# Compressing the prompt's blocks together with the last cached chunk, and re-measured durations in the build-time planner

## The chip, the cores and the metric

One core of a Trainium2 chip runs the whole program. The metric is the device time of one execution in microseconds (us). The engines are TensorE (PE, with its weight loads listed apart as PEld), VectorE (DVE), ScalarE (ACT), GpSimd (POOL) and SyncE (SP), which issues all DMA transfers here.

## The reference, cut to what matters

The reference runs two layers of a hybrid decoder on a prompt (512 tokens) and on eight samples of four tokens, with shared weights. Per layer:

```python
h = rmsnorm(x, norm_g) * (1 + scale) + shift
u, z_s5, q, kvx, gate_logits, z_nsa, merge_logits = split(h @ w_in)
y5 = s5_scan(u, ...); y5 = gelu(y5); y5 = y5 * sigmoid(y5 @ glu_w + glu_b) * silu(z_s5)
kc = rope(silu((kv_all[0] blocks of 64 + pe) @ cmp_w1[0]) @ cmp_w2[0])   # compressed keys
vc =      silu((kv_all[1] blocks of 64 + pe) @ cmp_w1[1]) @ cmp_w2[1]    # compressed values
o  = gated sum of attention over compressed, selected and window keys
out = (m_s5 * (y5 @ w_s5_out) + m_nsa * ((o * silu(z_nsa)) @ w_nsa_out)) @ w_o
x = x + gate * out
```

For the samples, `kv_all` is 2048 cached rows, read through a page table (16 pages for each of 8 samples and layer), and the new rows. For the prompt it is the prompt's own 512 rows, 8 blocks. One `rmsnorm(x, final_g)` ends the program.

## The kernel before, in words

Activations lie transposed (features on partitions, 512 + 32 tokens along the free axis), cut at token 256 into two halves h = 0 and 1. The wide matrices are split into a high and a low part, and each product is three matmuls. Weight blocks of 128 x 1024 are streamed by DMA (`w_dma`), their high part is cast on ACT (`w_hi`) and the low part subtracted on DVE (`w_lo`), a block ahead of use.

The order of instructions on every engine is fixed at build time. Each piece of work (dense projections, S5 set-up and tiles, compression, attention of the prompt, of the samples, modulation, stores) is a Python generator, a thread with a priority (a lower number goes first; the dense thread has 50, the last). `_Sched.run` resumes the best thread that is ready; what it emits goes to the end of its engine's queue. A thread waits by `yield ev(...)` (something has been emitted), `yield w_` (all that it last emitted is done by the model), or for memory, which `alloc` takes from one arena in SBUF. When things are done is told by a model, `_Clock.note`, which gives each instruction a duration; nothing of these waits exists on the chip, where semaphores alone hold an engine back.

Compression (`compress(l)`): a thread of its own loads the cached pages in eight chunks of 16 pages. For each chunk `products` runs 64 matmuls (32 steps x keys and values) against the resident first weights `cw1`, with 64 columns (4 for each page), 68 in the first chunk, where the encoding `pe` is a 17th page that gives the bias. Then come a bias addition on DVE, a tanh on ACT and `hidden` on DVE. After all chunks `keys` and a value matmul make `kcT` and `vc`. In layer 1 it starts when layer 0's attention is done, and chunk 5 and later ones wait for the end of layer 0.

The prompt's own blocks went separately: dense blocks 14 and 15 (`job_kv`, `post_c`) write the prompt's raw keys and values into four pages `cpage`, and after all projections, in layer 1 also after `compress(1)`, `compress_new(l)` loads `cw1` (2 x 1 MB) and `pe` again, runs the same 64 products with 20 columns, and makes `kcbd` and `vcbd`. The prompt's attention (`prompt`) waits for both, for the projections and for `cmp`.

`s5_wa`, four times a layer, makes its matrices with six DVE operations of 512 columns (a strided operand among them) and then transposes them on PE.

The end: `wo` has eight output blocks; in the last layer `final(h)` multiplies by `final_g` and the reciprocal norm, six blocks on DVE with one scalar_tensor_tensor each, two on POOL after a scaling on DVE, and stores them in pairs.

Of the kernel before, what the change touches and what calls it, by code (L numbers as in the profile page):

```python
# [21 lines left out]
P = 128  # L22
# [81 lines left out]
class _Clock:  # L104
# [41 lines left out]
    def note(self, e, op, args, kw):  # L146
# [44 lines left out]
        elif op == "dma_start":  # L191
            h = self.free[e] = t0 + 0.45
            d = max(self.free.get("dma", 0.0), h + 0.65)
            n = max(x.free_size() * x.ap[0][1] for x in views[:2]) / P if out.space != DRAM else out.free_size() * out.ap[0][1] / P
            end = self.free["dma"] = d + n * 1.42e-3 + 0.01
            vis = end + 0.78
        else:
            extra = 0.061 * sum(1 for x in ins[1:] if x.free_size() == 1) if e == "dve" else 0.0
            if e == "dve":
                c = 0.068 + n * (0.0063 if op == "reciprocal" else 0.00052 if op in ("tensor_scalar", "tensor_copy", "memset") and out.space != PSUM and all(x.space != PSUM for x in ins)  # L200
                                 else 0.00104) + extra
            elif e == "act":
# [88 lines left out]
def body(ctx: ExitStack, tc: tile.TileContext, A, O):  # L291
# [84 lines left out]
    class Ring:  # L376
# [371 lines left out]
    def dense(l):  # L748
# [95 lines left out]
        cpb = q["cpb"] = yield from alloc(5 * 256)  # L844
        cpage = q["cpage"] = cpb.v(5, 2, 32, 4)
# [32 lines left out]
        def job_kv(i):  # L878
            fmb = misc.next()
# [23 lines left out]
            def post_c(h):  # L903
                if h == 0:
                    return
                ty = i - 14
                store(O["kv"][l, ty], fm, fmb)
                for q2 in range(2):
                    ps = psq()
                    for qq in range(2):  # L910
                        qs = slice((2 * q2 + qq) * P, (2 * q2 + qq + 1) * P)
                        tr(ps[:, qq * 256:qq * 256 + P], fm[:, qs])
                        tr(ps[:, qq * 256 + P:qq * 256 + 256], fxs[0][:, qs])

                    pv = ps.rearrange("p (q s g d e) -> p q s g d e", q=2, s=2, g=2, e=2)
                    for d2 in range(2):
                        pr = slice(d2 * 64, d2 * 64 + 64)
                        for half in range(2):
# [205 lines left out]
        def final(h):  # L1124
            a, b = HALVES[h]
            yield ev("rstd", l, h)
            for k in range(8):
# [6 lines left out]
                if k % 2:  # L1134
                    sp.dma_start(O["y"][:, k - 1:k + 1, a:b], yb.v(8, N)[:, k - 1:k + 1, a:b])
        early = (0, 1)
        w = {}
        for m, h in [(m, h) for m in range(6) for h in range(2)] + [(6, 0), (7, 0), (6, 1), (7, 1)]:
# [21 lines left out]
            elif h == 1:  # L1160
                square_acc(acc, xn(m), m)
            if m == 7:
# [5 lines left out]
                else:  # L1168
                    if h == 0:
                        yb = yield from alloc(8 * N)  # L1170
                        for k in early:
                            dve.tensor_scalar(yb.v(8, N)[:, k], xn(k), C["final_g"][:, k:k + 1], None, op0=ALU.mult)
                    S.spawn(final(h), 4, "y")
            yield t()
# [422 lines left out]
    def compress(l):  # L1597
# [3 lines left out]
        kcT, vc, cw2, pbias = q["kcT"], q["vc"], q["cw2"], q["kcb"].v(1, at=1040)  # L1601
        cwb = []
        for _ in range(2):
            cwb.append((yield from alloc(2048, True, keep)))
        cw1 = [b.v(32, 64) for b in cwb]
        ckb = []
        for _ in range(CKB[l]):
            ckb.append((yield from alloc((NPG + 1) * 256, True, keep)))
        hb = yield from alloc(512 + 64 * 2 + 256, True, keep)
        hid = hb.v(8, 2, 32)  # L1610
        xb, th, kt1 = hb.v(64, at=512), hb.v(64, at=576), hb.v(8, 32, at=640)
        for ty in range(2):
            sp.dma_start(cw1[ty], A["cw1"][l, :, ty])

        def loads():
            for c in range(NB):
                if c >= CKB[l]:
                    yield ev("ck", l, c - CKB[l])
                ck = ckb[c % CKB[l]].v(NPG + 1, 2, 32, 4)
                if c == 0:  # L1620
                    sp.dma_start(ck[:, NPG].rearrange("p t d c -> p (t d c)"), A["pe4"][l])
# [5 lines left out]
                yield "for", [], [ck]  # L1627
# [5 lines left out]
        for c in range(NB):  # L1633
            if l > 0 and c == CMP_LATE:
                yield ev("x", l - 1)
            yield ev("ckl", l, c)
            ck = ckb[c % CKB[l]].v(NPG + 1, 2, 32, 4)
            npx = NPG + (c == 0)
            yield from products(ck, cw1, npx, B[7])
            done("ck", l, c)  # L1640
            if c == 0:
                dve.tensor_copy(pbias, B[7][:, 64:65])
            dve.tensor_scalar(xb, B[7][:, 0:64], pbias, None, op0=ALU.add)
            act.activation(th, xb, AF.Tanh, scale=0.5)
            hidden(hid, c, 32, th, xb)
        yield w_
        yield from keys(kcT, kt1, cw2, hid, 0, 8, 32, B[7])
# [7 lines left out]
        for b in ckb + cwb + [hb]:  # L1655
            b.free()
        done("cmp", l)

    def compress_new(l):

        q = L[l]
        yield from compressed_of(l)
        cw2 = q["cw2"]
        kcbd = q["kcbd"] = q["kcb"].v(2, 8, at=512)
        vcbd = q["vcbd"] = q["kcb"].v(8, 64, p=64, at=528)
        if l == 0:
            yield ev("s5m", l)
        cwb = []
        for _ in range(2):
            cwb.append((yield from alloc(2048, True)))  # L1670
        cw1 = [b.v(32, 64) for b in cwb]
        hb = yield from alloc(64 + 32 * 2 + 16 + 64 + 64 + 1, True)
        pbias = hb.v(1, at=272)
        hid, xb, th = hb.v(1, 2, 32), hb.v(32, at=64), hb.v(32, at=96)
        kc, kt1, hrep, vcr = hb.v(1, 8, at=128), hb.v(1, 8, at=136), hb.v(4, 2, 8, at=144), hb.v(64, p=64, at=208)
        for ty in range(2):
            sp.dma_start(cw1[ty], A["cw1"][l, :, ty])
        yield w_
        sp.dma_start(q["cpage"][:, 4].rearrange("p t d c -> p (t d c)"), A["pe4"][l])
        yield w_  # L1680
        yield from products(q["cpage"], cw1, 5, B[4])
        dve.tensor_copy(pbias, B[4][:, 16:17])
        dve.tensor_scalar(xb[:, 0:16], B[4][:, 0:16], pbias, None, op0=ALU.add)
        act.activation(th[:, 0:16], xb[:, 0:16], AF.Tanh, scale=0.5)
        hidden(hid, 0, 8, th, xb)
        yield w_
        yield from keys(kc, kt1, cw2, hid, 0, 1, 8, B[4])
        pool.memset(kcbd, 0.0)
        for g in range(2):
            dve.tensor_copy(kcbd[g * 64:g * 64 + 64, g, :], kc[g * 64:g * 64 + 64, 0, :])  # L1690
        dve.tensor_copy(hrep, hid[:, 0:1, :, 0:8].to_broadcast([P, 4, 2, 8]))
        yield w_
        pe.matmul(B[4][0:64, 0:64], hrep[64:128].rearrange("p r g n -> p (r g n)"), cw2[64:128, 0, :],
                  start=True, stop=True)
        act.activation(vcr, B[4][0:64, 0:64], AF.Copy, scale=0.5)
        dve.tensor_tensor(vcbd, vcr[:, None, :].to_broadcast([64, 8, 64]),
                          C["bd8"][0:64, :, None].to_broadcast([64, 8, 64]), op=ALU.mult)
        for b in cwb + [hb, q["cpb"]]:
            b.free()
        done("kcbd", l)  # L1700
# [385 lines left out]
    def main():  # L2086
# [268 lines left out]
```

## Time and profile before

| what | us |
|---|---|
| median of 3 runs | 1265.72 (1264.18 to 1266.66) |
| profiled execution, its own time | 1271.5 |
| its span | 1269.6 |
| PE busy | 1167.3 |
| DVE busy | 780.0 |
| ACT busy | 473.2 |
| POOL busy | 159.6 |

The mean granted clock of PE is 0.956 of 2.4 GHz. A busy PE is not PE at its peak: at half the clock the same matmuls are busy for twice as long.

### The profile page before, as it was taken

To read this page: it belongs to the slowest core of one execution; us is meant where nothing else is said; L and a number is where in the kernel's file an instruction comes from. 1 tells how busy PE (TensorE), PEld (TensorE's weight loads), DVE (VectorE), ACT (ScalarE), POOL (GpSimd) and SP (SyncE) were. 2 spreads that over 40 slices of the span, in tenths; PEclk is the share of its full clock that TensorE was granted. 3 is DMA by queue.
4 is the path that set the end of the run, shared out by engine and by line. 5 is a ranking of instruction groups with operands and counts; after the bars stand their busy time and mean duration, and the time that the engine had idled before them with its cause. 6 is when DMAs were issued, how large, how long until landed. Compare 5 with 4: busy or idle time off the path is not lost.

```text
span 1269.6 us, 30887 instructions
## 1 busy us (share of the span) xinstructions
PE 1167.3 (92%) x11958; PEld 1057.9 (83%) x11958; DVE 780.0 (61%) x1793; ACT 473.2 (37%) x1122; POOL 159.6 (13%) x335
## 2 busy tenths in 40 slices
PE   5999898998999999999898889899999899999995
PEld 3788897987888888888787889888998778889994
DVE  4686765525666666557234588875756576664744
ACT  4434232313444445532123333242445444443321
POOL 0142242100000000000000232251200000000001
PEclk8999888987999999999899999989999999999997
DMA  9665545765556747259888744645577555723742
GB/s 386 236 197 174 160 129 155 221 230 174 201 151 184 231 126 210 85 207 329 293 302 290 250 129 146 179 124 197 189 216 213 162 185 155 216 77 105 248 128 79
DMA packets 175156, 243.54 MB, mean 192 GB/s; under 512 B 33313, under 2 KB 129826, under 8 KB 172706
## 3 DMA queue, kind: packets, MB, share of 16 engines
q1 hardware_dynamic: 175010, 241.58, 59.6%
q8 instruction: 94, 1.54, 0.5%
q14 instruction: 52, 0.43, 0.1%
HBM read 211.86 MB, written 37.98 MB: 197 GB/s over the span
## 4 chain that ended last, share of the span: by engine, by line
PE 57%; DVE 16%; DMA 13%; SPq 5%; ACT 4%; issue 3%; DVEq 0%; ACTq 0%
PE bank L229 57%; DVE m L229 16%; SPq L229 4%; ACT m L229 3%; DMA m<-in_wblk 2%; DMA m<-in_wo 2%; DMA m<-kpd 1%; DMA m<-in_cmp 1%; DMA m<-in_xT 1%; DMA yd<-m 1%; DMA m<-in_cw 1%; DMA kpd<-m 1%; DMA x_mid<-m 1%; DMA m<-mn 0%; DMA ms<-m 0%
## 5 line engine op out<-in xcount | busy, mean ns | idle before, releaser
L229 PE MATMUL bank<-m,m 128*128 128x288 f32 (+11 forms) x10796 | 1069.2, 282 | 48.7 <-DVE m L229 30.0
L229 PEld LDWEIGHTS bank<-m,m 128*128 128x128 f32 (+4 forms) x10796 | 966.8, 169 | 123.9 <-issue 46.0
L229 DVE TENSOR_TENSOR m<-m,m 128x256 f32<-128x256 f32 (+15 forms) x623 | 382.6, 636 | 163.4 <-ACT m L229 139.6
L229 ACT COPY m<-bank 128x128 f32<-128x128 f32 (+7 forms) x258 | 99.8, 399 | 313.3 <-PE bank L229 300.1
L229 ACT CAST m<-m 128x1024 fp32r<-128x1024 f32 (+7 forms) x274 | 174.9, 650 | 97.8 <-DVE m L229 57.0
L229 PE MATMUL bank<-c_k,m 128*128 128x128 f32 (+1 forms) x590 | 92.8, 281 | 21.8 <-DVE m L229 19.9
L229 ACT ACTIVATE m<-m 128x64 f32<-128x64 f32 (+6 forms) x76 | 35.2, 469 | 172.9 <-DVE m L229 164.9
L229 PEld LDWEIGHTS bank<-c_k,m 128*128 128x128 f32 x590 | 67.8, 145 | 34.2 <-DVE m L229 25.3
L229 ACT ACTIVATE m<-bank 128x256 f32<-128x256 f32 (+3 forms) x130 | 49.9, 389 | 88.4 <-PE bank L229 83.7
L229 POOL TENSOR_TENSOR m<-m,m 128x32 f32<-128x32 f32 (+4 forms) x100 | 56.2, 581 | 201.5 <-ACT m L229 175.1
L229 POOL CAST m<-m 64x128 fp32r<-64x128 f32 x64 | 24.1, 377 | 453.2 <-ACT m L229 429.9
L229 ACT ACTIVATE m<-bank,m 128x384 f32<-128x384 f32 (+4 forms) x132 | 67.8, 522 | 13.0 <-DVE m L229 13.0
L229 DVE TENSOR_REDUCE m<-bank 128x1 f32<-128x128 f32 (+4 forms) x132 | 57.2, 473 | 16.6 <-PE bank L229 16.1
L229 DVE COPY m<-bank 128x32 f32<-128x32 f32 (+6 forms) x104 | 39.2, 384 | 40.6 <-PE bank L229 22.9
L229 DVE SCALAR_TENSOR_TENSOR m<-m,bank 128x256 f32<-128x256 f32 x96 | 41.4, 433 | 32.6 <-PE bank L229 13.3
L229 DVE SCALAR_TENSOR_TENSOR m<-m,m 128x256 f32<-128x256 f32 (+5 forms) x64 | 28.3, 466 | 45.1 <-ACT m L229 44.6
L229 DVE TENSOR_SCALAR m<-m,m,m 128x128 f32<-128x128 f32 (+4 forms) x132 | 52.5, 439 | 2.5
L229 POOL TENSOR_TENSOR m<-m,c_k 128x256 f32<-128x256 f32 (+2 forms) x32 | 34.0, 1062 | 150.4 <-PE bank L229 150.2
L229 POOL MEMSET m<- 128x32 f32 (+5 forms) x52 | 8.2, 180 | 266.6 <-PE bank L229 179.2
L229 DVE SCALAR_TENSOR_TENSOR m<-bank,mod,m 128x256 f32<-128x256 f32 x32 | 15.2, 480 | 40.7 <-PE bank L229 28.3
L229 ACT ACTIVATE m<-m,m 128x512 f32<-128x512 f32 (+2 forms) x24 | 15.9, 662 | 58.9 <-DVE m L229 53.8
L229 ACT ACT_TABLE_LOAD x24 | 30.8, 1283 | 16.1 <-DVE m L229 15.0
(60 smaller groups left out, 413.7 us busy)
## 6 DMA issues: line engine op xcount, KB each, us to landing
m<-in_wblk SPq DMA_DIRECT2D x78, 512.0 KB, 4.4
m<-in_cmp SPq DMA_DIRECT2D x256, 128.0 KB, 3.5
m<-in_kvsel SPq DMA_DIRECT2D x256, 128.0 KB, 3.0
m<-in_ada_w SPq DMA_DIRECT2D x32, 512.0 KB, 4.8
m<-in_ada_q SPq DMA_DIRECT2D x8, 1024.0 KB, 14.7
m<-in_cw SPq DMA_DIRECT2D x8, 1024.0 KB, 7.5
m<-in_wo SPq DMA_DIRECT2D x16, 512.0 KB, 5.6
ms<-m SPq DMA_DIRECT2D x16, 272.0 KB, 3.1
```

Of the source, the lines that this page charges most:

```text
L229: return f(*args, **kw)
```

## The change

- In the model, DVE's fixed part becomes 0.155 us instead of 0.068 and a column 0.001 (0.0015 where an operand is strided by 8 or more, 0.0019 in a scan, 0.00055 for simple operations from SBUF to SBUF); POOL's fixed part is 0.27 instead of 0.12 and a column 0.0027 instead of 0.0022.
- `compress_new` is gone. `compress` takes chunk buffers of 21 pages instead of 17; the last four are `cpage`, into which dense blocks 14 and 15 write (block 14 waits until that buffer exists). Each chunk buffer gets `pe` once. The last chunk waits for block 15, has 84 columns, and its upper 20 give the prompt's blocks; from them `kcbd` and `vcbd` are made, ahead of the cached `kcT` and `vc`. The buffers are freed one by one.
- At the end, x times `final_g` is made on ACT as each block comes (`scaled`), `final` is a plain tensor_tensor on DVE or POOL, waits until the last output block has been emitted, and stores in the order 2, 4, 0, 6.
- `job_kv` waits until the next two of three scratch buffers are not held by a store.

```diff
-                c = 0.068 + n * (0.0063 if op == "reciprocal" else 0.00052 if op in ("tensor_scalar", "tensor_copy", "memset") and out.space != PSUM and all(x.space != PSUM for x in ins)
-                                 else 0.00104) + extra
+                far = any(abs(x.ap[-1][0]) >= 8 and x.ap[-1][1] > 1 for x in ins)
+                fast = op in ("tensor_scalar", "tensor_copy", "memset") and all(x.space != PSUM for x in [out] + ins)
+                c = 0.155 + extra + n * (0.0063 if op == "reciprocal" else 0.0019 if op == "tensor_tensor_scan" else
+                                         0.00055 if fast else 0.0015 if far else 0.001)
...
-                c = 0.12 + n * (0.0035 if op == "tensor_copy" else 0.0009 if op == "memset" else 0.0022)
+                c = 0.27 + n * (0.0035 if op == "tensor_copy" else 0.0009 if op == "memset" else 0.0027)
...
+        def wait(self, n):
+            while any(self.b[(self.i + 1 + j) % len(self.b)] in kept for j in range(n)):
+                yield t(0.3)
...
+                if i == 15:
+                    done("cp", l)
+            if i == 14:
+                yield ev("ckb", l)
...
-                if k in early:
-                    pool.tensor_tensor(yk, yk, rr[:, a:b], op=ALU.mult)
-                else:
-                    dve.scalar_tensor_tensor(yk, xn(k)[:, a:b], C["final_g"][:, k:k + 1], rr[:, a:b],
-                                             op0=ALU.mult, op1=ALU.mult)
+            yield ev("last", l)
...
+                (pool if k < 2 else dve).tensor_tensor(yk, yk, rr[:, a:b], op=ALU.mult)
...
+        def scaled(m, a, b):
+            act.activation(yb.v(8, N)[:, m, a:b], xn(m)[:, a:b], AF.Identity, scale=C["final_g"][:, m:m + 1])
...
+            last = c == NB - 1
+            if last:
+                yield ev("cp", l)
             yield ev("ckl", l, c)
-            npx = NPG + (c == 0)
+            npx = NPG + 5 if last else NPG + (c == 0)
...
+            n = 84 if last else 64
...
+            if last:
+                hidden(hnew, 0, 8, th[:, 68:84], xb[:, 68:84])
...
+        yield from keys(kc, kt2, cw2, hnew, 0, 1, 8, B[7])
...
+        done("kcbd", l)
...
         yield from keys(kcT, kt1, cw2, hid, 0, 8, 32, B[7])
...
-    def compress_new(l):
...
-            if l:
-                yield ev("cmp", l)
-            S.spawn(compress_new(l), 8, "cmpnew")
```

## Rows read from the trace of the kernel before

**Rows 1.** The page, engines: busy us (share of the span), instructions.
```profile
PE 1167.3 (92%) x11958; PEld 1057.9 (83%) x11958; DVE 780.0 (61%) x1793; ACT 473.2 (37%) x1122; POOL 159.6 (13%) x335
```

**Rows 2.** Busy times by stretch: length, busy by engine, granted clock, DMA share, GB/s.
```profile
72.00:262.00 190.00, 174.49 (x2051) 166.96 (x2052) 118.15 (x204) 60.47 (x114) 55.49 (x94) 0.94 0.58 172
262.00:312.00 50.00, 43.02 (x492) 39.46 (x491) 21.37 (x64) 12.97 (x31) 5.01 (x17) 0.78 0.58 190
312.00:560.00 248.00, 241.80 (x2376) 210.09 (x2375) 155.41 (x403) 111.84 (x317) 9.80 (x28) 0.99 0.53 167
560.00:690.00 130.00, 117.41 (x1516) 107.81 (x1514) 56.58 (x132) 33.35 (x62) 0.31 (x4) 0.96 0.92 314
690.00:905.00 215.00, 196.28 (x1950) 183.03 (x1950) 162.16 (x326) 78.06 (x161) 63.80 (x124) 0.95 0.56 175
905.00:1240.00 335.00, 327.37 (x3052) 296.86 (x3052) 208.78 (x521) 144.34 (x377) 12.71 (x39) 0.99 0.56 172
```

**Rows 3.** Waits, whole program: who waited for whom, us, times, longest.
```profile
PE bank L229 <- DVE m L229: 69.5, 48, 12.1
```

**Rows 4.** Groups of PE's matmuls by shape: busy us, mean ns, idle before them.
```profile
L229 PE MATMUL bank<-m,m 128*64 128x64 f32 x1792 | 56.9, 226 | 5.2 <-DMA m<-in_cmp 5.2
L229 PE MATMUL bank<-m,m 128*64 128x20 f32 x256 | 10.9, 244 | 0.0
L229 PE MATMUL bank<-m,m 128*64 128x68 f32 x256 | 8.0, 223 | 0.6 <-issue 0.4 <-DMA ud<-m 0.2
```

**Rows 5.** Timeline, layer 0, 262 to 276.5 us: start, us, instruction, idle before it.
```profile
262.69 0.81 SPq L229 DMA_DIRECT2D m<-in_cw  x2
263.60 0.38 SPq L229 DMA_DIRECT2D m<-in_wblk  x1
...
273.55 1.04 ACT L229 CAST m<-m 128x1024 fp32r<-128x1024 f32 x1 [10.44 <-DMA m<-in_wblk]
...
274.78 0.23 DVE L229 SCALAR_TENSOR_TENSOR m<-m,m 128x64 f32<-128x64 f32 x1 [6.48 <-ACT m L229]
...
275.06 1.65 PE L229 MATMUL bank<-m,m 64*64 64x256 f32 x8 [2.30 <-DVE m L229]
```

**Rows 6.** Busy times of one stretch of layer 0.
```profile
275.00:295.00 20.00, 19.89 (x219) 17.40 (x220) 7.91 (x18) 2.96 (x8) 2.40 (x13) 0.57 0.41 136
```

**Rows 7.** Timeline of PE: matmuls with an identity that waited for DVE.
```profile
72.18 0.55 PE L229 MATMUL bank<-c_k,m 128*128 128x128 f32 x3 [2.00 <-DVE m L229]
...
846.88 0.23 PE L229 MATMUL bank<-c_k,m 32*32 32x32 f32 x1 [2.28 <-DVE m L229]
862.99 0.55 PE L229 MATMUL bank<-c_k,m 128*128 128x128 f32 x3 [2.10 <-DVE m L229]
```

**Rows 8.** Groups of DVE's operations by shape.
```profile
L229 DVE TENSOR_TENSOR m<-m,m 128x512 f32<-128x512 f32 x56 | 50.8, 933 | 6.0 <-DMA gd<-m 5.3
...
L229 DVE TENSOR_TENSOR m<-m,m 128x288 f32<-128x288 f32 x14 | 6.4, 458 | 2.5 <-ACT m L229 2.2
```

**Rows 9.** Timeline of the end, and the group of the last multiplies.
```profile
1251.35 2.64 PE L229 MATMUL bank<-m,m 128*128 128x288 f32 x18
...
1252.09 3.42 DVE L229 SCALAR_TENSOR_TENSOR m<-m,c_k,m 128x256 f32<-128x256 f32 x6
...
1255.43 0.47 DVE L229 SCALAR_TENSOR_TENSOR m<-bank,mod,m 128x256 f32<-128x256 f32 x1
...
1258.98 0.18 DVE L229 RECIPROCAL rsc<-rsc 128x3 f32<-128x3 f32 x1 [1.73 <-ACT rsc L229]
...
L229 DVE SCALAR_TENSOR_TENSOR m<-m,c_k,m 128x288 f32<-128x288 f32 x6 | 3.8, 701 | 2.0 <-ACT m L229 2.0
```

**Rows 10.** Timeline, layer 1: store of block 15, and compress_new's bias copy and last multiply.
```profile
779.93 0.53 SPq L229 DMA_DIRECT2D out_kv<-m  x1
...
872.31 0.16 DVE L229 COPY m<-bank 128x1 f32<-128x1 f32 x1 [4.74 <-PE bank L229]
...
892.84 0.68 DVE L229 TENSOR_TENSOR m<-m,c_k 64x512 f32<-64x512 f32 x1
```

More of the change, by code (lines that the diff above doesn't have):

```diff
@@ L843, in dense @@
         gtok = q["gtok"] = vtb.v(5, 32, at=1280)
-        cpb = q["cpb"] = yield from alloc(5 * 256)
-        cpage = q["cpage"] = cpb.v(5, 2, 32, 4)
         ropeC, ropeS, swap = C["ropeC"], C["ropeS"], C["swap"]
@@ L878, in job_kv @@
         def job_kv(i):
+            yield from misc.wait(2)
             fmb = misc.next()
@@ L905, in post_c @@
                     return
-                ty = i - 14
+                ty, cpage = i - 14, q["cpage"]
                 store(O["kv"][l, ty], fm, fmb)
@@ L1126, in final @@
             yield ev("rstd", l, h)
-            for k in range(8):
+            yield ev("last", l)
+            for k in (0, 1, 2, 3, 4, 5, 6, 7):
                 yk = yb.v(8, N)[:, k, a:b]
-                if k in early:
-                    pool.tensor_tensor(yk, yk, rr[:, a:b], op=ALU.mult)
-                else:
-                    dve.scalar_tensor_tensor(yk, xn(k)[:, a:b], C["final_g"][:, k:k + 1], rr[:, a:b],
-                                             op0=ALU.mult, op1=ALU.mult)
-                if k % 2:
-                    sp.dma_start(O["y"][:, k - 1:k + 1, a:b], yb.v(8, N)[:, k - 1:k + 1, a:b])
-        early = (0, 1)
+                (pool if k < 2 else dve).tensor_tensor(yk, yk, rr[:, a:b], op=ALU.mult)
+            for k in (2, 4, 0, 6):
+                sp.dma_start(O["y"][:, k:k + 2, a:b], yb.v(8, N)[:, k:k + 2, a:b])
+        def scaled(m, a, b):
+            act.activation(yb.v(8, N)[:, m, a:b], xn(m)[:, a:b], AF.Identity, scale=C["final_g"][:, m:m + 1])
         w = {}
+        if l + 1 == DEPTH:
+            yb = yield from alloc(8 * N)
         for m, h in [(m, h) for m in range(6) for h in range(2)] + [(6, 0), (7, 0), (6, 1), (7, 1)]:
@@ L1161, in dense @@
                 square_acc(acc, xn(m), m)
+            if (m, h) == (7, 1):
+                done("last", l)
             if m == 7:
@@ L1168, in dense @@
                 else:
[L1169 to L1172, printed above, removed]
                     S.spawn(final(h), 4, "y")
+            if l + 1 == DEPTH:
+                if m >= 6:
+                    scaled(m, a, b)
+                elif h == 1:
+                    scaled(m, 0, N)
             yield t()
@@ L1601, in compress @@
         kcT, vc, cw2, pbias = q["kcT"], q["vc"], q["cw2"], q["kcb"].v(1, at=1040)
+        kcbd, vcbd = q["kcbd"], q["vcbd"] = q["kcb"].v(2, 8, at=512), q["kcb"].v(8, 64, p=64, at=528)
         cwb = []
@@ L1607, in compress @@
         for _ in range(CKB[l]):
[L1608 to L1611, printed above, removed]
+            ckb.append((yield from alloc((NPG + 5) * 256, True, keep)))
+        cks = [b.v(NPG + 5, 2, 32, 4) for b in ckb]
+        hb = yield from alloc(512 + 256 + 84 * 2 + 64 + 8 * 2 + 64 * 2, True, keep)
+        hid, kt1 = hb.v(8, 2, 32), hb.v(8, 32, at=512)
+        xb, th = hb.v(84, at=768), hb.v(84, at=852)
+        hnew, kc, kt2, hrep, vcr = (hb.v(1, 2, 32, at=936), hb.v(1, 8, at=1000), hb.v(1, 8, at=1008),
+                                    hb.v(4, 2, 8, at=1016), hb.v(64, p=64, at=1080))
         for ty in range(2):
             sp.dma_start(cw1[ty], A["cw1"][l, :, ty])
+        for ck in cks:
+            sp.dma_start(ck[:, NPG].rearrange("p t d c -> p (t d c)"), A["pe4"][l])
+        q["cpage"] = cks[(NB - 1) % CKB[l]][:, NPG + 1:NPG + 5]
+        done("ckb", l)
         def loads():
@@ L1618, in loads @@
                     yield ev("ck", l, c - CKB[l])
-                ck = ckb[c % CKB[l]].v(NPG + 1, 2, 32, 4)
-                if c == 0:
-                    sp.dma_start(ck[:, NPG].rearrange("p t d c -> p (t d c)"), A["pe4"][l])
+                ck = cks[c % CKB[l]]
                 for i in range(0, NPG, 4):
@@ L1626, in loads @@
                     yield t(PG_LAT)
-                yield "for", [], [ck]
+                yield "for", [], [ck[:, 0:NPG + 1]]
                 yield t(CK_LATE)
@@ L1635, in compress @@
                 yield ev("x", l - 1)
+            last = c == NB - 1
+            if last:
+                yield ev("cp", l)
             yield ev("ckl", l, c)
-            ck = ckb[c % CKB[l]].v(NPG + 1, 2, 32, 4)
-            npx = NPG + (c == 0)
-            yield from products(ck, cw1, npx, B[7])
+            npx = NPG + 5 if last else NPG + (c == 0)
+            if last:
+                yield "for", [], [cks[c % CKB[l]][:, NPG + 1:]]
+            yield from products(cks[c % CKB[l]], cw1, npx, B[7])
             done("ck", l, c)
+            for b in ([ckb[c % CKB[l]]] if c + CKB[l] >= NB else []) + (cwb if last else []):
+                b.free()
             if c == 0:
                 dve.tensor_copy(pbias, B[7][:, 64:65])
-            dve.tensor_scalar(xb, B[7][:, 0:64], pbias, None, op0=ALU.add)
-            act.activation(th, xb, AF.Tanh, scale=0.5)
-            hidden(hid, c, 32, th, xb)
+            n = 84 if last else 64
+            dve.tensor_scalar(xb[:, 0:n], B[7][:, 0:n], pbias, None, op0=ALU.add)
+            act.activation(th[:, 0:n], xb[:, 0:n], AF.Tanh, scale=0.5)
+            if last:
+                hidden(hnew, 0, 8, th[:, 68:84], xb[:, 68:84])
+            hidden(hid, c, 32, th, xb)
+        yield w_
+        yield from keys(kc, kt2, cw2, hnew, 0, 1, 8, B[7])
+        pool.memset(kcbd, 0.0)
+        for g in range(2):
+            dve.tensor_copy(kcbd[g * 64:g * 64 + 64, g, :], kc[g * 64:g * 64 + 64, 0, :])
+        dve.tensor_copy(hrep, hnew[:, 0:1, :, 0:8].to_broadcast([P, 4, 2, 8]))
+        yield w_
+        pe.matmul(B[7][0:64, 0:64], hrep[64:128].rearrange("p r g n -> p (r g n)"), cw2[64:128, 0, :],
+                  start=True, stop=True)
+        act.activation(vcr, B[7][0:64, 0:64], AF.Copy, scale=0.5)
+        dve.tensor_tensor(vcbd, vcr[:, None, :].to_broadcast([64, 8, 64]),
+                          C["bd8"][0:64, :, None].to_broadcast([64, 8, 64]), op=ALU.mult)
+        done("kcbd", l)
         yield w_
@@ L1654, in compress @@
             yield w_
-        for b in ckb + cwb + [hb]:
-            b.free()
+        hb.free()
         done("cmp", l)
-    def compress_new(l):
[L1661 to L1700, printed above, removed]
     def prompt(l):
```

## The prediction

> **What bounds the kernel now.** I read the page's engine table first, then the busy times by stage, PE's waits, and the timeline where PE stands still. The reader is to see that TensorE (PE) is busy nearly all the time [rows 1], so the span is PE's work, plus the stretches in which PE stands still, plus the stretches in which it runs at the lower of its two clock levels. The stage rows [rows 2] separate these. PE's idle time in the six stages is 15.5, 7.0, 6.2, 12.6, 18.7 and 7.6 us, together 67.6. Span times (1 − granted clock) is 11.4, 11.0, 2.5, 5.2, 10.8 and 3.4 us, together 44.3, which is the full-speed time that the 1.2 GHz level takes away. The two go together: the stages with idle time are those with a low clock. The totals of waits say for whom PE stands still: VectorE (DVE) ends 69.5 us of it [rows 3], 12.1 of them at the program's start.
>
> **Part A, the separate compression goes.** Per layer, compress_new loaded 2 x 1 MB of weights and a 128 KB block again and ran 64 products of 20 columns, two records each. In the trace they are 256 records, 10.9 us [rows 4], all in PE's own order, so all of it counts. In exchange the last cached chunk has 84 columns instead of 64. A chunk of 64 takes 56.9/14 = 4.1 us (1792 records, 128 a chunk). If its time grows with the columns, 20 more cost 4.1 x 20/64 = 1.3 us a layer. The 68-column chunks cost 8.0/2 = 4.0, no more than 64 columns, so the other end is 0. I take the dear end: −10.9 + 2.5 = −8.4 us (bounds −10.9 and −8.4). The small matmuls, the tanh and the copies behind the products remain; only their place changes.
>
> **Part B, the stall in layer 0 that the second weight load makes.** The order in the timeline [rows 5]: SyncE issues the two weight loads at 262.69; a dense weight block issued at 263.60, behind them, makes ScalarE (ACT) wait 10.44 us at 273.55; behind that cast stands the tanh of the last chunk, behind the tanh DVE's multiply at 274.78, and behind this the key matmuls, for which PE idles 2.30 us. From 275 to 295 the clock is then 0.57 [rows 6]: 8.6 us of full-speed time lost. Part A already holds some of it: of the 10.9 us, layer 1 can have taken some 4.1 (a whole chunk), so layer 0 took 6.8, 2.7 of them slowness. Remaining: 2.3 + 8.6 − 2.7 = 8.2 us. The loads go, but the key matmuls still stand behind a tanh in ACT's queue. I take two thirds, −5.5 (bounds 0 and −8.2).
>
> **Part C, waits that a wrong duration made.** The emission decides at build time when PE's next instruction may be put into its queue, which runs in order: if it thinks DVE done too early, dense matmuls stand behind a waiting one. The old model gives a 512-column DVE operation 0.068 + 512 x 0.00104 = 0.600 us; measured is 0.933 [rows 8]; the new one gives 0.155 + 512 x 0.0015 = 0.923 when the operand is strided. s5_wa puts six of these ahead of its transposes: the plan is early by 6 x 0.333 = 2.0 us. That is what the trace shows: the waits before those transposes are 2.00 us at 72.18, 2.10 at 862.99 [rows 7], and 2.28, 2.31, 2.08 and 1.10 at the four between, 11.9 us in six. I expect two thirds to go, since the dense blocks can fill the place: −7.9. Of what else waits for DVE, 69.5 − 12.1 − 11.9 − 2.3 (part B) = 43.2 us, such as the 2.28 at 846.88 [rows 7], some is of this kind and some is real dependence, as at the start of attention or at the layer's seam. I take an eighth, −5.4. Together −13.3 (bounds 0 and −11.9 − 43.2/4 = −22.7).
>
> **Part D, the clock behind them.** Outside part B's stage, 60.6 us of idle time goes with 33.3 us lost to the clock [rows 2]. If 13.3 of the 60.6 go, 22% of 33.3 is −7.3 (bounds 0 and, with 22.7, −12.5).
>
> **Part E, the end.** Now the six h = 0 multiplies hold DVE from 1252.09, so the evacuation of the last matmuls, which end at 1251.35 + 2.64 = 1253.99, starts at 1255.43 [rows 9]: 1.4 us late. The change puts those six behind the evacuation, and so ahead of or beside the second rstd, in which DVE idles only 1.73 us before its reciprocal. If they take 3.42 us as now, they cost 3.4 − 1.7 = 1.7. The net is +0.3. The six 288-column multiplies of the last half are 701 ns each beside POOL's two [rows 9], against 458 for the same size elsewhere [rows 8]; a two-operand tensor_tensor beside the same two POOL multiplies I price like the row beside POOL, no gain. The other end is 458 ns: −6 x 0.243 = −1.5 for the last half, and 0.9 less for the first, so bounds −2.1 and +0.3, and I take +0.3. The scaling that moves to ACT lies under wo, where ACT is busy 144 of 335 us [rows 2]; without that cover it would be ten operations, some 5 us. Stores of y: the same eight on SyncE, four of them later; the last still follows the last multiply.
>
> On this one the Trainium skill ("SBUF — State Buffer", section "SBUF: two separate sides") has a rule that speaks against the change. It says that VectorE and GpSimd share one port pair under an exclusive lock, which a VectorE operation with two SBUF inputs needs too while GpSimd reads SBUF, so that one of them stands still. The 701 against 458 ns agrees in direction. By that rule part E is +0.3, without it −2.1.
>
> **Costed at nothing.** The wait of layer 1's last chunk for block 15 is one of the emission's thread, not of an engine: block 15 is stored at 779.93 [rows 10], and until then the dense thread feeds PE. Without that cover it would cost the chunk, 5 us. PE's queue then has dense matmuls behind the chunk, and what it waits for on the chip is the last copies of ACT and DVE, a wait of the 2 us kind. The buffers held until then (weights, one chunk) compete with the S5 tiles for SBUF; counting the allocations I find room for the first tile. Key and value work of the prompt now stands ahead of "cmp", on which the sample, the attention and the second modulation load depend: one chain later. Dense gate blocks hide it; if they ran out it would cost up to the 20 us that it takes beside dense work in layer 1, from 872.31 to 892.84 [rows 10]. The poll in misc.wait (0.3 us a step) is hidden the same way.
>
> **Sum.** B + C + D = −26.1. A new order also makes waits that are not there now; no row sizes them, so their bounds are 0 and all of 26.1. I give back 40%, +10.4: the idle time that the change doesn't touch (60.6 − 13.3 = 47.3) is over three times what it takes away, and its places are drawn anew. −8.4 − 26.1 + 0.3 + 10.4 = −23.8 us. Against the profiled execution, 1271.5 us (span 1269.6), that is 1247.7; the median of the runs is 1265.72, 0.5% less, and from there 1242.
>
> **The rivals.**
> Rival 1: the durations move the order but not the waits; only A and part of B count. −8.4 − 5.5 + 0.3 = −13.6: 1252. For it: most waits on DVE are dependences. Against it: 2.0 us worked out and 2.00 to 2.31 measured.
> Rival 2: nothing is given back, and the far ends of A and E hold: −10.9 − 26.1 − 2.1 = −39: 1227, or lower where more of C goes. For it: six equal waits with one cause. Against it: every order has to fill the same gaps with the same dense blocks.
> Rival 3, slower: in layer 1 the prompt's attention no longer waits for its compressed values, whose last multiply is at 892.84, but starts with the end of the projections at 846.88 [rows 10, 7]. In that stage DVE is busy 162 of 215 us [rows 2], and S5 tiles are still in it. If six of the 32 attention units come to lie in those 46 us, and each stops PE at its two places (transposes behind normalise, the value matmuls behind the copies) by 2.2 us as s5_wa's transposes do, and the clock takes half as much again, that is 12 x 3.3 = 40 us against the 23.8: +16, so 1282. It decides from 23.8/12 = 2 us a place, clock included. Against it: the plan now prices DVE in full and would hold these units back.
> Rival 4: gains and new waits cancel, 1266.
>
> **Chances.** Forecast (own range 1231 to 1249) 0.47; rival 1 0.22; rival 2 0.10; rival 4 0.07; rival 3 0.14. A measurement of this kernel can tell about 0.2% (2.5 us) from no change. Faster by more than that: 0.47 + 0.22 + 0.10 = 0.79; within: 0.07; slower: 0.14. The range 1222 to 1267 takes in rivals 1, 2 and 4 and leaves out rival 3 and the far end of C and D.
>
> **What would show it.** A: no 20-column records, 256 records of 84 columns with 4.1 to 5.4 us per 128. B: no ACT wait of 10 us near 263 to 274, and no 20 us at half clock after it. C: the waits before the four-transpose groups under 0.5 us, and PE's total for DVE near 55. D: the mean clock at 0.965 or above instead of 0.956. E: the last evacuation straight behind its matmuls, and the second reciprocal late by 1 to 2 us. The prediction is wrong if PE's idle time between 72 and 1240 us does not fall by 5 us or more, or if new waits of 2 us stand between 846 and 905.

## The result, and the profile after

Four runs of each: 1244.55 us (1241.83 to 1249.9) after, 1266.19 (1264.18 to 1269.35) before; ratio 0.9837 [0.9805, 0.9869], 21.6 us faster. The forecast was 1242. The profiled execution took 1244.75 us, its span is 1243.0; the page's engine line:

```profile
PE 1142.0 (92%) x11702; PEld 1037.6 (83%) x11702; DVE 780.4 (63%) x1787; ACT 481.5 (39%) x1130; POOL 154.8 (12%) x335
```

Against [rows 1] the span is 26.6 us shorter, PE's busy time 25.3 shorter, and its idle time nearly unchanged (102.3 before, 101.0 now). The 256 matmuls that went are the 20-column records. Most of the rest is clock: span x (1 − mean granted clock) was 1269.6 x 0.044 = 55.9 us and is 1243.0 x 0.033 = 41.0.

Each trace is one execution, and that of before is one with a low clock: 0.956, where its 66 other runs in the experiments below have 0.964 in the mean (0.954 to 0.972). By those runs before loses 44.9 us to the clock and not 55.9. The changed kernel loses 38.5 us in its four runs and 42.2 in six of `old_tail`, which has its order up to the last blocks. So the clock gave 2 to 6 of the 21.6 us, and not the 14.9 that the two traces show.

The forms, to be held against [rows 4], and the four-transpose groups (the last row here; the first row of the second fence is before's):

```profile
L231 PE MATMUL bank<-m,m 128*64 128x64 f32 x1536 | 51.2, 232 | 12.3 <-DMA m<-in_cmp 5.6 <-DMA m<-in_ada_w 5.3 <-issue 1.4
L231 PE MATMUL bank<-m,m 128*64 128x84 f32 x256 | 9.7, 237 | 0.0
L231 PE MATMUL bank<-m,m 128*64 128x68 f32 x256 | 9.6, 246 | 5.4 <-DMA ud<-m 3.5 <-DMA m<-in_cmp 1.9
L231 PE MATMUL bank<-c_k,m 128*128 128x128 f32 x524 | 77.6, 278 | 4.4 <-DVE m L231 2.8 <-ACT m L231 1.4
```

```profile
L229 PE MATMUL bank<-c_k,m 128*128 128x128 f32 x524 | 80.6, 282 | 17.9 <-DVE m L229 16.8 <-ACT m L229 0.7
```

The products together take 70.5 us instead of 75.8. The wait of 128 x 128 transposes for DVE fell from 16.8 to 2.8 us. PE's waits as a whole (us, times, longest; the first row answers to [rows 3]), after and then those of before that are not in [rows 3]; what no engine or transfer ended (1.4 us after, 2.1 before) and 0.2 us of before for `ud` are left out:

```profile
PE bank L231 <- DVE m L231: 48.8, 28, 12.1
PE bank L231 <- ACT m L231: 14.6, 17, 3.3
PE bank L231 <- DMA m<-in_ada_w: 8.0, 5, 5.3
PE bank L231 <- DMA m<-in_cmp: 7.5, 5, 3.3
PE bank L231 <- DMA m<-ud: 4.3, 3, 1.9
PE bank L231 <- DMA ud<-m: 3.5, 1, 3.5
PE bank L231 <- POOL m L231: 2.3, 1, 2.3
PE bank L231 <- DMA m<-kpd: 1.6, 2, 0.8
```

```profile
PE bank L229 <- ACT m L229: 11.4, 15, 3.3
PE bank L229 <- DMA m<-in_cmp: 5.2, 4, 2.2
PE bank L229 <- DMA m<-kpd: 2.5, 3, 1.7
PE bank L229 <- DMA m<-ud: 2.4, 3, 1.5
```

For DVE PE waits 20.7 us less, for DMA 24.9 instead of 10.3, for ACT 3.2 more and for POOL 2.3: 20.1 together, nearly what DVE gave. That is why the idle time did not move.

**Where the time went.** Stages by the clock on the wall no longer hold the same work, so the borders are now events: the first and the last matmul that adds the causal mask in the prompt's attention (two to a unit, 32 units a layer). In order: 72 us to attention of layer 0, that attention, the seam to attention of layer 1, that attention, the rest. Columns: length, PE busy (instructions), granted clock, DMA share, GB/s. Before, then after:

```profile
72.00:323.35 251.35, 228.87 (x2661) 0.90 0.58 177
323.35:547.90 224.55, 218.35 (x2144) 0.99 0.54 168
547.90:911.98 364.08, 332.77 (x3649) 0.96 0.68 223
911.98:1142.27 230.29, 223.03 (x2192) 0.99 0.58 176
1142.27:1269.60 127.33, 112.70 (x883) 0.93 0.45 140
```

```profile
72.00:286.74 214.74, 204.41 (x2513) 0.99 0.62 187
286.74:524.00 237.26, 231.12 (x2290) 0.99 0.60 184
524.00:840.52 316.52, 277.37 (x3046) 0.93 0.66 215
840.52:1130.68 290.16, 281.41 (x2703) 0.99 0.57 172
1130.68:1243.00 112.32, 97.84 (x769) 0.93 0.45 144
```

The lengths can't be compared alone, since dense work moves between stages; what a stage loses can: its idle time, and its length x (1 − clock). Ahead of layer 0's attention the loss was 22.5 + 25.1 = 47.6 us and is 10.3 + 2.1 = 12.4: 35.2 us gained, two thirds of it clock. In the seam it was 31.3 + 14.6 = 45.9 and is 39.1 + 22.2 = 61.3: 15.4 given back. The other stages move by 1 to 2 us. Idle time and clock loss together fall by some 16 us over the span (1.3 + 14.9); the other 10.4 of the 26.6 us are PE's busy time at full clock, of which the products give some 6 (part A below) and the rest has no place.

How far do such losses go without any change of order? Up to 250 us `before_cwlate` (below) issues the same instructions in the same order as before. From 72 to 250 us, in before and then in `before_cwlate`:

```profile
72.00:250.00 178.00, 162.82 (x1944) 0.93 0.57 170
72.00:250.00 178.00, 161.14 (x1978) 0.97 0.58 175
```

The idle time is 15.2 and 16.9 us, the clock loss 12.5 and 5.3. `old_tail` has the order of the changed kernel up to the last blocks; the same two stages in it:

```profile
72.00:284.92 212.92, 202.60 (x2491) 1.00 0.61 189
...
522.84:834.29 311.45, 276.22 (x3046) 0.94 0.66 219
```

They lose 10.3 and 53.9 us, against 12.4 and 61.3. So a stage can differ by some 7 us between two executions of one order, and some 5 of the 35.2 us ahead of attention are of this kind, 7 of them clock less 2 of idle time. The experiments below are read by these two losses; a difference of less than some 8 us between two traces shows nothing by itself.

### The profile page after: what moved, and what is told of

It reads as the page before. It is cut to its first block, busy times and chain, and to the rows that moved or that the text cites. A ratio compares the mean times of both kernels' runs of the same rounds, so it can differ in the third digit from the quotient of the medians.

```text
span 1243.0 us, 30351 instructions
## 1 busy us (share of the span) xinstructions
PE 1142.0 (92%) x11702; PEld 1037.6 (83%) x11702; DVE 780.4 (63%) x1787; ACT 481.5 (39%) x1130; POOL 154.8 (12%) x335
## 4 chain that ended last, share of the span: by engine, by line
PE 69%; DMA 11%; DVE 7%; ACT 4%; SPq 4%; issue 2%; POOL 0%; DVEq 0%; ACTq 0%; POOLq 0%
PE bank L231 69%; DVE m L231 7%; SPq L231 3%; ACT m L231 3%; DMA m<-in_cmp 2%; DMA m<-in_cw 2%; DMA yd<-m 1%; DMA m<-in_ada_w 1%; DMA m<-kpd 1%; DMA m<-ud 1%; DMA m<-yd 1%; DMA m<-in_s5k 0%; DMA m<-in_wo 0%; ACT L231 0%; DMA gd<-m 0%
## 5 line engine op out<-in xcount | busy, mean ns | idle before, releaser
L231 PE MATMUL bank<-m,m 128*128 128x256 f32 (+13 forms) x10540 | 1048.2, 283 | 62.5 <-DVE m L231 26.6
L231 DVE TENSOR_TENSOR m<-m,m 128x1024 fp32r<-128x1024 f32 (+15 forms) x635 | 386.2, 630 | 156.8 <-ACT m L231 129.6
L231 ACT CAST m<-m 128x1024 fp32r<-128x1024 f32 (+5 forms) x274 | 174.2, 650 | 89.3 <-DVE m L231 62.8
L231 ACT COPY m<-bank 128x512 f32<-128x512 f32 (+7 forms) x258 | 100.1, 400 | 268.0 <-PE bank L231 258.4
L231 ACT ACTIVATE m<-m 128x544 f32<-128x544 f32 (+8 forms) x74 | 34.7, 476 | 186.0 <-DVE m L231 171.8
L231 PE MATMUL bank<-c_k,m 128*128 128x128 f32 (+2 forms) x590 | 88.8, 277 | 5.0 <-DVE m L231 2.8
L231 ACT ACTIVATE m<-bank 128x288 f32<-128x288 f32 (+4 forms) x130 | 50.4, 390 | 104.5 <-PE bank L231 103.8
L231 PEld LDWEIGHTS bank<-c_k,m 128*128 128x128 f32 (+1 forms) x590 | 68.0, 145 | 15.0 <-DVE m L231 5.2
L231 ACT ACTIVATE m<-bank,m 128x128 f32<-128x128 f32 (+4 forms) x132 | 67.8, 523 | 14.4 <-DVE m L231 11.4
L231 DVE TENSOR_REDUCE m<-bank 128x1 f32<-128x128 f32 (+4 forms) x132 | 57.3, 474 | 18.6 <-PE bank L231 17.9
L231 DVE COPY m<-bank 128x32 f32<-128x32 f32 (+6 forms) x102 | 39.1, 389 | 46.4 <-ACT m L231 24.7
L231 DVE SCALAR_TENSOR_TENSOR m<-m,bank 128x256 f32<-128x256 f32 x96 | 41.5, 434 | 41.2 <-ACT m L231 25.1
L231 DVE TENSOR_SCALAR m<-m,m,m 128x128 f32<-128x128 f32 (+3 forms) x132 | 52.5, 439 | 2.5
L231 DVE SCALAR_TENSOR_TENSOR m<-bank,mod,m 128x256 f32<-128x256 f32 x32 | 15.4, 482 | 34.9 <-PE bank L231 21.3
```

Source lines behind the costliest of these rows:

```text
L231: return f(*args, **kw)
```

## The experiments

Every ratio is to runs of the kernel before on the same chip.

**One half of the change alone.** `model_only` is before with the new durations, `old_model` is the changed kernel with the old ones:

```diff
 # model_only = before, and in _Clock.note
+                far = any(abs(x.ap[-1][0]) >= 8 and x.ap[-1][1] > 1 for x in ins)
+                fast = ...
+                c = 0.155 + extra + n * (... 0.00055 if fast else 0.0015 if far else 0.001)
+                c = 0.27 + n * (... 0.0027)
 # old_model = the reverse of these hunks in the changed kernel
```

> The kernel before with the new durations for VectorE and GpSimd alone; compression, tail and waits as before. Theory 1 (accurate durations take waits of TensorE for VectorE away): part C and D less what is given back, -13.3 - 7.3 + 8.2 = -12.4 us, so about 1254, TensorE's total wait for VectorE down from 69.5 to about 50 us. Rival (a new order is only another draw): 1266 within 5 us, that total between 60 and 80. Rival (the gain is the saved compression): 1266.

> The changed kernel with the durations of before: joint compression, new tail and scratch-buffer wait, but the old plan's prices. Theory (the saved products count in full, part A -8.4, B -5.5 with 2.2 given back, E 0.3): about -11.4 us, so 1255. Rival (all of it is the durations): 1266. Waits before the four-transpose groups come back at about 2 us each.

Measured: `model_only` 1274.44 us, ratio 1.0096 [1.0063, 1.0128], slower. `old_model` 1260.08, ratio 0.9974 [0.9946, 1.0003], no change that can be told. The sizes expected were wrong for both: +1.0% and −0.3% alone, −1.6% together. This does not show that the gain needs both halves, since each time is also that of one order (see the five nanoseconds below). PE's total wait for DVE is 60.3 us in `model_only`, where about 50 was expected. Yet the mechanism of part C is there, in the four-transpose groups of `model_only` and `old_model`:

```profile
L231 PE MATMUL bank<-c_k,m 128*128 128x128 f32 x524 | 78.5, 280 | 5.7 <-DVE m L231 3.6 <-ACT m L231 2.1
```

```profile
L229 PE MATMUL bank<-c_k,m 128*128 128x128 f32 x524 | 80.6, 284 | 14.4 <-DVE m L229 12.8 <-ACT m L229 1.4
```

The waits of about 2 us are there with the old durations and gone with the new ones: this row's wait for DVE is 12.6 to 21.4 us in the five traces with the old durations, and 1.5 to 6.2 in the nine with the new.

`model_only` loses 21.8 us ahead of layer 0's attention instead of 47.6, and 64.0 in the seam instead of 45.9. What it loses in layer 0's attention stands at the end of that stage, in PE's timeline (start, us, ..., idle before it):

```profile
525.52 2.21 PE L231 MATMUL bank<-m,m 128*64 128x128 f32 x20 [1.14 <-DVE m L231]
530.30 2.21 PE L231 MATMUL bank<-m,m 128*64 128x128 f32 x20 [1.14 <-DVE m L231]
```

The last dense block there is stored at 502.17, the last unit of attention begins at 545.76 (before: 567.96 and 547.9). Five units follow each other at 4.2 to 4.9 us with no dense work between, and PE waits for DVE in each; in before the last ones follow at 8 to 10 us. I call such units bare. The attention stage loses 18.9 us instead of 8.4. My reading, which no run shows: with the old durations dense work stood behind the waits, was used up later, and still covered this place. In the changed kernel attention starts 37 us earlier, and two units are bare:

```profile
517.68 2.22 PE L231 MATMUL bank<-m,m 128*64 128x128 f32 x20 [1.13 <-DVE m L231]
521.95 2.21 PE L231 MATMUL bank<-m,m 128*64 128x128 f32 x20 [1.04 <-DVE m L231]
```

**The tail, and the second weight load.** `old_tail` is the changed kernel with the end of before; `before_cwlate` is before with layer 0's second weight load held back:

```diff
 # old_tail, final(h): the changed kernel's lines taken out, before's put back
-            yield ev("last", l)
-                (pool if k < 2 else dve).tensor_tensor(yk, yk, rr[:, a:b], op=ALU.mult)
+                    dve.scalar_tensor_tensor(yk, xn(k)[:, a:b], C["final_g"][:, k:k + 1], rr[:, a:b],
 ...
 # before_cwlate, compress_new
         if l == 0:
             yield ev("s5m", l)
+            yield ev("cmp", l)
```

> The changed kernel with the final multiplies of before (scalar_tensor_tensor ahead of the last evacuation, stores in order). Part E by the prediction: +0.3, so 0.3 us faster than the changed kernel, 1244. By the trace of after, the last matmul to the end of the span took 1243.0 - 1228.6 = 14.4 us against 1269.6 - 1254.0 = 15.6 before: 1.2 us slower, 1246. Either is under the resolution of the time; the profile decides: 14.4 or 15.6 from the last block's matmuls to the end.

> The kernel before, with the separate compression of layer 0 started only after the cached one is finished, so that its two weight loads no longer stand ahead of the dense weight block in the queue. Part B: the ACT wait of 10.4 us and the 20 us at half clock go, -5.5 us (up to -8.2), so about 1260. Rival (the stall is the key chain's own, or comes back later when the loads are issued): 1266, or up to 1270, as the prompt's attention starts later by the load.

Measured: `old_tail` 1243.28 us, 0.9848 [0.9807, 0.989]: the tail is worth nothing that can be told in the time. Its trace decides as was asked: from the end of the last block's matmuls, at 1217.9, to the end of the span, at 1233.6, it takes 15.7 us, as before. `before_cwlate` 1282.14, 1.0161 [1.0121, 1.02]: slower where −5.5 was expected. The stall itself went: no ACT wait of 10 us, the 20-column products at 7.8 instead of 10.9 us, the loss ahead of attention 25.0 instead of 47.6. But attention starts 9 us later, five of its units are bare (loss 14.0 instead of 8.4), and the seam loses 67.5 us instead of 45.9. Together that is 27.2 us lost against 22.6 won, by two traces: that of `before_cwlate` is its fastest run, 1276.47, and that of before is slower than its median. At least 5 of the 22.6 lie ahead of 250 us, where the order is still the same.

**When attention starts.** The changed kernel with layer 0's attention put back by 38 us of the planner's time:

```diff
         for e in ("qkv", "kcbd"):
             yield ev(e, l)
+        if l == 0:
+            yield t(38)
```

> The changed kernel, but the prompt's attention of layer 0 starts 38 us later by the planner's time (behind kcbd), about where it starts before the change. Theory (the joint compression pays because attention starts 37 us earlier and so still has dense blocks beside it at its end): 4 to 6 units of layer 0 run without dense work, each costing 1 to 2 us of waiting for DVE and a lower clock, and the time is 1252 to 1260. Rival (the start of attention is of no account, the gain is the work that is gone): 1244, within 3.

Measured: 1272.5 us, 1.0041 [1.0015, 1.0067]. The direction is as expected, the size beyond it: the whole gain is gone. Its first three stages:

```profile
72.00:326.37 254.37, 237.95 (x2840) 0.98 0.63 191
326.37:549.71 223.34, 209.01 (x2058) 0.98 0.54 166
549.71:882.34 332.63, 287.22 (x3116) 0.93 0.65 210
```

Five bare units instead of two: the attention stage loses 18.8 us instead of 8.5, the 10.3 that the theory had priced. 9.1 more go ahead of attention and 7.4 in the seam, which it had not. So three more bare units go with some 10 us here; but the edit also draws a new order, and that the start of attention is the cause is not shown.

**How much of 22 us is this one order?** Five nanoseconds on one constant change no data dependence and no operation, but for two or four table loads of ACT in some, only the order that the emission works out:

```diff
-                c = 0.155 + extra + ...     # the changed kernel
+                c = 0.150 + extra + ...     # after_150; 0.160 and 0.145 likewise
-                c = 0.068 + ...             # before
+                c = 0.063 + ...             # before_063; 0.073 likewise
```

> The changed kernel with one constant moved: DVE's fixed part in the model is 0.150 us instead of 0.155 (5 ns for each instruction, less than the spread of the measured durations). Theory 1 (the gain comes from the accuracy of the new durations and from the joint compression): 5 ns change nothing, 1244 us, within 4. Theory 2 (any change of a duration draws the order of the dense filler and of the attention anew, and the order that is drawn is worth some ten us either way): the time leaves 1244 by more than 6 us, to the slow side more likely than not, 1250 to 1265, and the trace shows attention units without dense work behind them at the end of layer 0 or 1 that the changed kernel does not have.

> The same with 0.160 us instead of 0.155. Theory 1: 1244 us, within 4. Theory 2: away from 1244 by more than 6 us, 1250 to 1265; if this one and the kernel with 0.150 both come near 1244, theory 2 falls.

> A third neighbour of the changed kernel: DVE's fixed part 0.145 us instead of 0.155. If 1244 us is the lucky one of the changed kernel's orders, this one is slower by 6 us or more, as 0.150 and 0.160 were (1269 to 1271); if those two were the unlucky ones, it comes within 4 us of 1244.

> The kernel before with one constant moved: DVE's fixed part in the old model is 0.063 us instead of 0.068. Theory 2 (the order drawn is worth some ten us either way, in any model): the time leaves the 1266 us of before by more than 5, to either side. Rival (only the new model, with its joint compression, stands on a narrow good order; the old one is indifferent): 1266, within 3. The two neighbours of before together say where before itself stands among its draws: if both are slower, its 1266 is a good draw too and the change's gain is real against like; if both are faster, part of the gain is before's bad draw.

> The same with 0.073 us instead of 0.068. Theory 2: away from 1266 us by more than 5. Rival: 1266, within 3.

| kernel | us | ratio to before | loss ahead of attention 0 | loss in the seam |
|---|---|---|---|---|
| before | 1266.19 | 1 | 47.6 | 45.9 |
| before_063 | 1283.7 | 1.017 [1.0127, 1.0214] | 23.0 | 83.6 |
| before_073 | 1275.44 | 1.0111 [1.0061, 1.0161] | 15.5 | 83.2 |
| after | 1244.55 | 0.9837 [0.9805, 0.9869] | 12.4 | 61.3 |
| after_145 | 1263.55 | 0.9993 [0.9962, 1.0024] | 19.1 | 73.2 |
| after_150 | 1271.29 | 1.0035 [1.0001, 1.0069] | 20.9 | 65.1 |
| after_160 | 1269.39 | 1.0009 [0.9979, 1.0038] | 9.0 | 75.7 |

(Us, ratio with its interval, each to before on the same chip, then idle time plus clock loss of two stages.) In the times theory 2 held five times out of five, and twice the time went beyond its 1265. Before and after are each the fastest among their neighbours. Best against best the change is worth 1.6%. The means of the two families, 1.0094 (three) and 0.9969 (four), are 1.2% apart, with a spread of 0.9% in each: the change's worth apart from the order is some 16 us by these few draws, and not sure to be above nothing.

The two halves lie with these families by their compression: `model_only` (1.0096) with the neighbours of before, `old_model` (0.9974) with those of the changed kernel, and with them the two means stay 1.0094 and 0.9970. Parted by durations instead, the means are 1.0064 and 0.9994. So what gain there is seems to go with the joint compression and not with the new durations; nine draws with a spread of 0.7 to 0.8% in each group don't show it.

Bare units at the end of layer 0's attention don't explain the neighbours: `after_150` and `after_160` have none there, so this sign of theory 2 did not come. What these two lose lies in the seam and behind layer 1's attention. The ahead-of-attention and seam stages of `before_063`, then those and the last stage of `after_160`:

```profile
72.00:320.12 248.12, 232.54 (x2809) 0.97 0.63 195
...
539.49:928.82 389.33, 333.03 (x3583) 0.93 0.64 206
```

```profile
72.00:283.67 211.67, 202.69 (x2512) 1.00 0.64 191
...
527.17:859.30 332.13, 283.02 (x3052) 0.92 0.65 211
...
1145.32:1262.90 117.58, 95.76 (x773) 0.89 0.39 126
```

The last stage loses 21.8 + 12.9 = 34.7 us in `after_160`, and 32.8 in `after_150`, where the changed kernel loses 22.3: in both PE waits for DVE twice for over 3 us behind the last unit, and in the changed kernel it does not.

The low clock ahead of attention (0.90) is in the trace of before alone, in part by that execution, as the rows up to 250 us show. `before_063` has the same second weight load and 0.97 there. And no other kernel has so small a loss in the seam as before. The long waits in the seam, in the changed kernel, then in `after_160`:

```profile
564.81 5.37 PE L231 MATMUL bank<-m,m 128*128 128x256 f32 x24 [5.14 <-DVE m L231]
...
662.92 1.21 PE L231 MATMUL bank<-ones,m 128*128 128x1 f32 x6 [3.04 <-DVE m L231]
685.00 8.80 PE L231 MATMUL bank<-m,m 128*64 128x64 f32 x152 [5.32 <-DMA m<-in_ada_w]
835.39 3.96 PE L231 MATMUL bank<-m,m 128*128 128x256 f32 x28 [5.11 <-DVE m L231]
```

```profile
567.00 6.75 PE L231 MATMUL bank<-m,m 128*128 128x256 f32 x36 [4.99 <-DVE m L231]
578.04 9.18 PE L231 MATMUL bank<-m,m 128*128 128x288 f32 x154 [4.29 <-DVE m L231]
675.34 6.47 PE L231 MATMUL bank<-m,m 128*64 128x64 f32 x128 [4.98 <-DMA m<-in_ada_w]
...
850.78 5.34 PE L231 MATMUL bank<-m,m 128*128 128x288 f32 x24 [4.97 <-DVE m L231]
```

Three are alike in both (564.81 and 567.00; 685.00 and 675.34; 835.39 and 850.78), the others are not. Which decision of the emission makes the seam good or bad was not found.

**Other fillers for the seam.** Both are the changed kernel; `after_cl4` holds back layer 1's compression from its fifth chunk on instead of its sixth, `after_fill4` also starts that compression beside the bare units:

```diff
-CMP_LATE = 5
+CMP_LATE = 4
 # after_fill4 also: compress(1) waits for ("mn", 0) and ("smp", 0) in place of ("att", 0),
 # and layer 0's attention uses PSUM bank 4 where the changed kernel goes over to bank 7
```

> The changed kernel with the fifth chunk of layer 1's compression, not the sixth, held back to the end of layer 0 (the constant CMP_LATE 4 instead of 5); the order up to the seam between the layers stays, and 64 products move from before the seam to behind it, where PE waits for wo's weights in 564 to 600 us less than it waits for the pages. Theory (the seam is the place with most idle time left, 11.6 us in 550 to 600 and 11.0 in 650 to 700): 1238 to 1242. Theory 2 (an edit of the order is as likely to lose): 1244 to 1262.

> The changed kernel, with compression of layer 1 started when layer 0's merge blocks and samples are emitted instead of after its whole attention (so its products stand beside the last units of attention, which have no dense block left), and its fifth chunk instead of the sixth held back to the end of layer 0. Theory (bare units and the seam between the layers are what is left to gain): 510 to 540 us keeps a clock of 0.95 or more instead of 0.87, the wait of 5.14 us at 565 goes, and the time is 1236 to 1240. Rival (the waits only move, or the earlier pages collide with the weights of wo): 1244 to 1250.

Measured: `after_cl4` 1241.06 us, 0.9821 [0.9771, 0.9871]; `after_fill4` 1247.29, 0.9859 [0.9813, 0.9905]. Neither can be told from the changed kernel, at 0.9837. The first came out in its theory's range, 1238 to 1242, and loses 50.7 us in the seam instead of 61.3; but `old_tail`, without that edit, loses 53.9 there, so the edit is not shown to have done it. The second removes the 5.14 us wait and loses 57.0 in the seam, but the clock from 510 to 540 us stays at 0.89, where 0.95 was expected. Both keep the changed kernel's order up to the seam (to 553 us and beyond), and both keep its gain.

## Why the prediction was right in its time, and where its steps failed

The time was hit in good part by luck. 1244.55 us is the time of one order; the three neighbours, with the same operations and durations within 10 ns, take 1263.55 to 1271.29, all outside the prediction's own range of 1231 to 1249.

**Part A, mis-sized.** −5.3 us instead of −8.4. The 10.9 us held 3.1 of low clock: where nothing stalls, the same 256 records take 7.8 (`before_063`, `before_cwlate`). The 84-column chunks cost 9.7 against 7.9 for two of 64 at full clock (47.6/12 x 2 in `old_model`), +1.8 where +2.5 was taken. At full clock that makes −6.0; the chunks of 64 and 68 columns hold the other 0.7 in low clock.

**Part B, right on what stood there, wrong on why.** The stall went. But `before_063` issues the same second load at 271.36 and has a clock of 1.00 from 262 to 320 us, where before has 0.57 from 275 to 295 [rows 6]. The load makes the stall only in the order of before.

**Part C, shown for the transposes, not for the time.** The six-operation error of 2.0 us makes waits of 2.0 us: 16.8 us of waiting with the old durations, 2.8 with the new. PE's total for DVE was expected near 55 and is 48.8, but 61.6 and 66.2 in `after_150` and `after_160`, so that total too is one order's. Nearly all that DVE gave came back as waits for DMA, ACT and POOL: the idle time did not fall by the 13.3 us of this part.

**Part D, large in the two traces, small over the runs.** Of the 26.1 us of B, C and D, 13.3 were idle time and 7.3 the clock behind it. Ahead of layer 0's attention idle time gave 12.2 and the clock 23.0 in the traces. The clock's gain is not in proportion to the idle time, as the step had it: 22.5 us of waiting in small pieces took 25.1 us at the low level, while 39.1 in the seam now take 22.2. But the trace of before holds some 11 us of low clock that its other runs don't have, and over the runs the clock gave 2 to 6 us. The sign asked for, a mean clock of 0.965 or above, was met with 0.967, and says little where before itself has 0.964.

**Part E, inside its bounds.** From the end of the last block's matmuls to the end: 1269.6 − 1253.99 = 15.6 us before, 1243.0 − 1228.63 = 14.4 now, −1.2 instead of +0.3. The timeline that answers to [rows 9]:

```profile
1226.80 1.83 PE L231 MATMUL bank<-m,m 128*128 128x288 f32 x12
...
1228.67 0.48 DVE L231 SCALAR_TENSOR_TENSOR m<-bank,mod,m 128x256 f32<-128x256 f32 x1 [1.84 <-PE bank L231]
...
1232.43 0.17 DVE L231 RECIPROCAL rsc<-rsc 128x3 f32<-128x3 f32 x1
...
1235.29 3.49 DVE L231 TENSOR_TENSOR m<-m,m 128x288 f32<-128x288 f32 x6 [2.04 <-ACT m L231]
1235.34 2.02 POOL L231 TENSOR_TENSOR m<-m,m 128x288 f32<-128x288 f32 x2 [6.33 <-ACT m L231]
```

The evacuation starts straight behind its matmuls, as forecast. The second reciprocal comes 3.76 us after the evacuation's start instead of 3.55, so it is late by 0.2 us where 1 to 2 were expected: the six first-half multiplies, priced at 3.42 us, lie in the 2.4 us before it. The last six multiplies take 3.49 us beside POOL's two: 582 ns each, against 458 for the size elsewhere [rows 8]. The Trainium skill ("SBUF — State Buffer", section "SBUF: two separate sides") says that VectorE and GpSimd hold a shared port pair by an exclusive lock, for the whole instruction. The trace agrees in direction only: standing still for all of POOL's 2.02 us would be, as an estimate, 6 x 0.458 + 2.02 = 4.8 us.

**The give-back, and the step that failed.** 10.4 us were given back without a place; 15.4 were, in the seam. The step that failed beside it is "Dense gate blocks hide it": the last is stored at 514.76, the last unit of attention begins at 524.0, and the seam begins bare. That this is what the seam lost by is not shown: `after_150`, with dense work up to its last unit, loses 65.1 us there. The condition that I had set for being wrong was met: between 72 us and the last stage's end (1240 before, 1213.4 now) PE's idle time went from 67.6 to 64.4 us, 3.2 and not 5. The other condition, new waits of 2 us between 846 and 905, was not: PE's longest there is 1.76 us. In the two traces the clock gave what the idle time did not; over the runs it gave 2 to 6 us, the products some 6, and for the other 10 to 14 of the 21.6 no place was found.

**The rivals.** Rival 1 (the durations move the order but not the waits, 1252) comes nearest to the means of the two families, 16 us apart: these seem to go with the compression, and PE's idle time did not move. Rival 3 (attention of layer 1 stops PE) fell: it starts at 840.52 instead of 911.98, and its stage idles 8.8 us instead of 7.3. Rival 4 (gains and new waits cancel, 1266) is what three of the four orders of the changed program show: most of the transposes' waits are gone in them too, and the time is not lower. That each of the two times is that of one order, worth some 1% either way, was in no rival.

## What to carry to other kernels

Where a build-time planner orders in-order queues, make an edit of a few nanoseconds to one of its constants and time that, before a gain of 1 or 2% is put down to what the edit does. Compare stages between events of the work, not between times, and add idle time and clock loss in each: here that showed a gain of 35 us in one stage and 15 lost in another behind a total idle time that did not move. Before such a difference is read, look at a second trace of the same order: here a stage moved by 7 us without any change, and the mean clock of one trace was 0.008 under that of the other runs. Filler work is a stock: in `model_only`, `before_cwlate` and `after_late` it ran out before layer 0's attention ended, and the stage lost 6 to 10 us more.

## What was not expected of the hardware

The clock's cost does not follow the idle time, and not the order of instructions alone. Before attention of layer 0, 22.5 us of idle time go with a granted clock of 0.90 in before, and 18.6 us with 0.99 in `after_150`: 25.1 against 2.3 us lost. And one order, run twice, gave 15.2 us of idle time at 0.93 and 16.9 us at 0.97 between 72 and 250 us. Why the clock differs between such executions is open.
